# Dealing a skinny fp32 projection to four column groups of TensorE's array

## The chip, the core and the metric

The kernel runs on one core of a Trainium2 chip. The metric is the device time of one execution in microseconds. Before the change three runs gave 2735.04, 2735.30 and 2738.25 us, median 2735.3. A profile of one further execution shows what each engine did and when: TensorE (PE, with its weight loads as PEld), VectorE (DVE), ScalarE (ACT), GpSimd (POOL) and SyncE (SP), which issues the DMAs.

## The reference

Two layers of a hybrid backbone over 2048 latent tokens and 256 context tokens of width 1024. Each layer normalises its input, modulates it by vectors that come from a conditioning vector, and runs windowed attention (8 heads) and a bidirectional mLSTM (4 heads) side by side, followed by one output projection:

```python
sc = jax.nn.silu(c)
scc = jax.nn.silu(c_ctx)
for l in range(DEPTH):
    mod_x = jnp.split((sc @ w_ada[l] + b_ada[l])[:, None, :], 3, axis=-1)
    mod_c = jnp.split(scc @ w_ada[l] + b_ada[l], 3, axis=-1)
    x, ctx = hybrid_layer(x, ctx, mod_x, mod_c, tables, norm_g[l], w_in[l], ...)
...
    xn = rmsnorm(x, norm_g) * (1 + scale_x) + shift_x
    cn = rmsnorm(ctx, norm_g) * (1 + scale_c) + shift_c
```

The change is in the two products with `w_ada[l]`, 1024 x 3072 in fp32: two rows (`sc` and `scc`) times a large matrix, once per layer.

## The kernel before

The kernel records its instructions through a planner (`Plan`): generators yield while something they need is not there yet by the planner's own model, and the loop `run_until` lets the next one go. `cost` holds the planner's price of every instruction; `stream` gives each large job a priority and a weight, and among equal priorities the job that has used the least planned TensorE time for its weight goes first. So the planner's prices set the order in which all engines' instructions stand, and each engine then runs them in that order, waiting on semaphores. All instructions carry the line of the helper `op`, L228 in the profile, so the rows are told apart by tiles and not by lines.

`ada` computes the modulation. Its columns are cut into chunks: 8 chunks of 256 columns in the first stretch (shift and scale of layer 0, buffers `wada`, of which there are three), and then 32 chunks of 128 columns (the gate of layer 0, all of layer 1, buffers `g`, shared with other work). For each chunk, `loads` issues the load of the weights `wt` (1024 rows as eight k-tiles of 128) and of the bias `bt`. Then eight matmuls, one for each k-tile, accumulate in one PSUM bank `b`: the stationary operand is `self.sc[:, k, :]`, 128 rows by two columns (latent and context), the moving operand is the k-tile of `wt`, 128 rows by 256 or 128 columns, and the result is two partitions of the bank. The generator `rows` then adds the bias on DVE, for the scale also multiplies by the norm's gain, takes a maximum for the scaling of fp16 splits (`gm`), and stores the row to `modD` in DRAM, from where it is loaded later, broadcast to 128 partitions (`kT`, `V`).

In the first stretch nothing else of size can run: the normalised input needs the modulation, and the loads of `x` (`xt<-in_x`) wait until the chunks are loaded and the context's rows are stored and loaded back. After that the 32 smaller chunks run as a stream of their own beside two large ones, the attention (`alpha`) and the mLSTM (`beta`). All work on layer 1 beyond its modulation starts after layer 0's output projection.

Of the kernel before, what the change touches and what calls it, by code (L numbers as in the profile page):

```python
# [10 lines left out]
ALU = mybir.AluOpType  # L11
# [4 lines left out]
KT = D // P  # L16
# [37 lines left out]
def _isap(v):  # L54
    return hasattr(v, "ap") and hasattr(v, "offset")


def _free(v):
    n = 1
    for d in v.shape[1:]:  # L60
        n *= d
    return n
# [33 lines left out]
def _move(out, in_):  # L96

    b = 2 if out.dtype == F16 else 4
    for d in out.shape:
        b *= d  # L100
    r = max(min(_run(out), _run(in_), 4096), 4)
    return b / r * (10 + 0.0447 * r) / 16e3


def _base(out, in_):

    if out.space == bass.MemoryType.DRAM:
        return 1.5
    return 1.9 if in_.name.startswith("in_") else 3.6
# [14 lines left out]
class Plan:  # L124
# [29 lines left out]
    def cost(self, e, name, a, kw):  # L154
        n = _free(a[0])
        if e == "E":
            if name == "transpose":
                return 0.003 + (n / 1200.0 if a[1].dtype == F32 else 0.03), 0.1
            if kw["rhs"].dtype == F32:
                return max(4 * n, 512) / 2400.0 + 0.005, 0.1  # L160
            return max(n, 64) / 2400.0 + 0.0027, 0.1
        if e == "Q":
            if name == "dma_start_transpose":
                return 1.2 + max(n - 512, 0) * 0.00045, 1.9 + n / 128 * 128 * 25e-3 / 16
            return 0.49, _base(a[0], a[1]) + _move(a[0], a[1])
        if name == "tensor_reduce":
            n = _free(a[1])
        cols = sum(_isap(v) and _free(v) == 1 for v in (*a[2:], kw.get("scale"), kw.get("bias")))
        if e == "S":
            base = 0.05 if a[1].space == bass.MemoryType.PSUM else 0.11  # L170
            return base + n / 1200.0 + 0.08 * cols + (0.11 if "accum_out" in kw else 0.0), LAT
        if e == "G":
            if name == "memset" or name == "tensor_copy":
                return 0.12 + n / 1600.0, LAT
            if name == "tensor_scalar":
                return 0.18 + n / 1080.0, LAT
            return (0.55 if a[-1] == ALU.pow else 0.14) + n * 2.1e-3, LAT
        if name == "reciprocal":
            n *= 8
        if name == "tensor_tensor_reduce":  # L180
            return 0.25 + n / 960.0, LAT
        if name == "tensor_copy" and a[0].dtype == F16:
            n /= 2
        return 0.065 * (1 + min(cols, 2)) + n / 960.0, LAT

    def op(self, e, name, fn, a, kw):
# [4 lines left out]
        if name == "tensor_tensor_reduce":  # L191
            outs.append(ins.pop())
        cost, lat = self.cost(e, name, a, kw)
        t = self.clk[e]
        for v in ins:
# [8 lines left out]
        if e == "Q":  # L204
            t = max(t, self.lanes.pop(0))
        elif e == "G" or (e == "V" and _two(a, kw)):
            other = self.port["V" if e == "G" else "G"]
            for p, q in other:
                if p <= t < q:
                    t = q  # L210
            self.port[e] = self.port[e][-5:] + [(t, t + cost)]
# [145 lines left out]
class Kern(Plan):  # L357
# [240 lines left out]
    def ada(self, l, parts, width, tags):  # L598

        A, Q, V = self.A, self.Q, self.V  # L600
        c = self.c
        nch = D // width
        if 1 not in parts:
            yield from self.need(("kv", l))
        else:
            gm = c.tile([2, 2, 8], F32, tag="gm", name="gm")
            V.memset(gm, 0.0)
        todo = [(j, n) for j in parts for n in range(nch)]
        ready = []

        def loads():
            for i, (j, n) in enumerate(todo):
                c0 = j * D + n * width
                if tags[0] == "g":
                    yield from self.room("g", 3)
                wt = yield from self.get(tags[0], [P, KT, width])
                Q.dma_start(wt, A["w_ada"][l, :, c0:c0 + width].rearrange("(k p) c -> p k c", p=P))
                bt = yield from self.get(tags[1])
                Q.dma_start(bt[:, 0], A["b_ada"][l:l + 1, c0:c0 + width].to_broadcast([2, width]))
                if j == 1:  # L620
                    Q.dma_start(bt[:, 1], A["norm_g"][l:l + 1, n * width:(n + 1) * width].to_broadcast([2, width]))
                ready.append((wt, bt))
                yield True
            if l == 0:
                self.done.add("ada in")

        def rows(j, n, ps, bt):
            row = yield from self.get(tags[2])
            yield from self.till(ps)
            V.tensor_tensor(row, ps[:2, :width], bt[:, 0], ALU.add)  # L630
            self.put(ps)
            if j == 1:
                V.scalar_tensor_tensor(row, row, 1.0, bt[:, 1], ALU.add, ALU.mult)
            self.put(bt)
            if j < 2:
                V.tensor_reduce(gm[:, 1 - j, n:n + 1], row, AX.X, ALU.max, apply_absolute_value=True)
            jj = {1: 0, 0: 1, 2: 2}[j]
            yield from self.till(row)
            for s in range(2):
                Q.dma_start(self.modD[l][s][jj][:, n * width:(n + 1) * width], row[s:s + 1])  # L640
            self.put(row)
            self.done.add(("mod", l, jj, n))

        self.spawn(loads())
        for i, (j, n) in enumerate(todo):
            while not ready:
                yield None
            wt, bt = ready.pop(0)
            yield from self.till(wt)
            ps = yield from self.get("b")  # L650
            for k in range(KT):
                self.mm(ps[:2, :width], self.sc[:, k, :], wt[:, k, :], start=(k == 0), stop=(k == KT - 1))
            self.put(wt)
            self.spawn(rows(j, n, ps, bt))
            yield True
            if (j, n) == (0, nch - 1):
                yield from self.need(*[("mod", l, a, b) for a in range(2) for b in range(nch)])
                bnd, mx = self.held(), self.held()
                V.memset(bnd, 0.0)
                m2 = self.col(2)  # L660
                V.tensor_reduce(m2[:2], gm, AX.X, ALU.max)
                V.tensor_tensor(bnd[:2], m2[:2, 0:1], m2[:2, 1:2], ALU.add)
                V.tensor_scalar(bnd, bnd, 32.0, None, ALU.mult)
                yield from self.pmax(bnd, mx)
                self.sx[l] = c.tile([P, 1], F32, name=f"sx{l}")
                self.ix[l] = c.tile([P, 1], F32, name=f"ix{l}")
                self.scale_of(mx, 1, self.sx[l], self.ix[l])
                self.done.add(("sx", l))
        yield from self.need(*[("mod", l, {1: 0, 0: 1, 2: 2}[j], n) for j, n in todo])
        if 0 in parts:  # L670
            self.done.add(("ada", l))
        if 2 in parts:
            self.done.add(("gate", l))
# [1361 lines left out]
```

## Time and profile before

| | us |
|---|---|
| median of three runs | 2735.3 |
| the profiled execution | 2737.6 |
| its span, first to last instruction | 2735.8 |
| PE busy in the span | 2445.0 (89%) |
| DVE busy | 1871.7 (68%) |
| ACT busy | 1496.5 (55%) |
| POOL busy | 1505.3 (55%) |

The page gives these shares; since the kernel runs in stages, the rows below are mostly of single stretches. A timeline row merges instructions of one kind that follow each other on one engine: start, length, engine, line, operation, output and input tiles, shapes, count, and in brackets the idle time before it with what ended it. A matmul's recorded length includes its way through the array, so consecutive ones overlap in the record; the pace of a run of n is its length less one record's, divided by n - 1, or the distance between the starts of two runs divided by the count.

### The profile page before, as it was taken

What the parts mean: (1) busy time and instruction counts of PE and PEld (TensorE: products, weight loads), DVE (VectorE), ACT (ScalarE), POOL (GpSimd) and SP (SyncE); (2) the same over time, 40 slices, a digit from 0 to 9 for tenths busy, and PEclk for the clock granted to TensorE, in tenths of its full rate; (3) what the DMA queues carried; (4) which work ended last, traced back from release to release, by engine and by line L of the source; (5) the groups of instructions that cost most, each with busy time, mean ns of one, the idle gap of its engine ahead of it and who ended that gap; (6) DMA issues with size and microseconds to landing.
All of it is one profiled execution on the core that took longest, in us unless ns stands there. A gap on an engine that the chain in (4) does not pass through costs nothing. (4 is left out here: it accounts for less than half of the span.)

```text
span 2735.8 us, 64752 instructions
## 1 busy us (share of the span) xinstructions
PE 2445.0 (89%) x23650; PEld 1883.3 (69%) x23650; DVE 1871.7 (68%) x4817; ACT 1496.5 (55%) x3788; POOL 1505.3 (55%) x2832
## 2 busy tenths in 40 slices
PE   6699999999999999886898799998899899978887
PEld 2567887789778968773454468968876896866333
DVE  4888666856685667576666687777659768666554
ACT  2446675657666756572222357756666676665111
POOL 1846477547765854574222664783786387357000
PEclk9799999999999999998999999999999999989998
DMA  8354873476457643687786437726754763466554
GB/s 269 96 157 98 162 142 86 117 157 135 85 141 157 137 109 91 127 194 207 183 197 189 111 96 158 144 58 126 153 117 104 140 126 83 98 150 152 159 161 123
DMA packets 822447, 376.16 MB, mean 137 GB/s; under 512 B 492536, under 2 KB 800240, under 8 KB 821104
## 3 DMA queue, kind: packets, MB, share of 16 engines
q1 hardware_dynamic: 822128, 372.02, 58.7%
q8 instruction: 186, 3.05, 0.5%
q14 instruction: 133, 1.09, 0.1%
HBM read 198.99 MB, written 57.56 MB: 94 GB/s over the span
## 5 line engine op out<-in xcount | busy, mean ns | idle before, releaser
L228 PEld LDWEIGHTS <-xt 128*128 128x128 f16 x12144 | 911.6, 99 | 303.6 <-issue 76.2
L228 PE MATMUL b<-woz,xt 128*128 128x256 f16 (+2 forms) x3872 | 496.1, 277 | 26.7 <-DMA xt<-xt 13.2
L228 PE MATMUL b<-xt,wqk 128*128 128x512 f16 (+1 forms) x1824 | 388.0, 363 | 2.7 <-DVE wqk L228 2.7
L228 POOL TENSOR_TENSOR held<-held,mhalf 128x1 f32<-128x1 f32 x200 | 117.8, 590 | 333.9 <-DVE held L228 321.4
L228 PEld LDWEIGHTS <-wqk 128*128 128x128 f16 x1824 | 174.8, 98 | 160.6 <-issue 4.3
L228 ACT ACTIVATE d<-d,smx,un 128x640 f32<-128x640 f32 (+2 forms) x272 | 223.9, 823 | 95.9 <-DVE smx L228 85.6
L228 DVE SCALAR_TENSOR_TENSOR ph<-d,ph 128x640 f16<-128x640 f32 (+2 forms) x272 | 211.9, 780 | 92.2 <-ACT ph L228 89.8
L228 PE MATMUL b<-wa,xt 128*128 128x128 f16 (+1 forms) x3352 | 259.6, 226 | 3.6 <-DVE held L228 1.1
L228 POOL TENSOR_TENSOR p<-p 128x128 f32<-128x128 f32 x272 | 127.2, 470 | 214.6 <-ACT p L228 165.4
L228 PE MATMUL b<-wv,xt 128*128 128x128 f16 x3456 | 229.7, 219 | 16.1 <-DVE s L228 6.2
L228 DVE CUSTOM_DVE_ANT_0 d<-d,mask 128x640 f32<-128x640 f32 (+1 forms) x240 | 195.9, 816 | 30.4 <-PE d L228 29.5
L228 POOL TENSOR_TENSOR g<-g,mb 128x512 f32<-128x512 f32 (+1 forms) x152 | 194.5, 1280 | 36.5 <-ACT g L228 21.5
L228 PE MATMUL b<-xt,xt 128*128 128x512 f16 x768 | 178.5, 395 | 33.6 <-ACT d L228 20.4
L228 PE MATMUL d<-ks,toz 128*128 128x256 f16 (+1 forms) x1568 | 189.2, 257 | 20.6 <-DVE toz L228 15.7
L228 POOL TENSOR_TENSOR toz<-toz,cs 128x256 f32<-128x256 f32 x160 | 119.7, 769 | 154.8 <-DMA cs<-in_rope 113.4
L228 PE MATMUL b<-xt,wa 128*128 128x256 f16 x1632 | 201.1, 273 | 2.3 <-DVE held L228 1.0
L228 ACT ACTIVATE ph<-d 128x640 f16<-128x640 f32 (+2 forms) x272 | 182.5, 671 | 14.3 <-DMA pp<-ph 7.2
L228 DVE TENSOR_TENSOR toz<-toz 64x256 f16<-64x256 f32 (+2 forms) x234 | 144.5, 618 | 60.7 <-ACT toz L228 28.5
L228 PEld LDWEIGHTS <-toz 128*128 128x128 f16 x1568 | 146.7, 99 | 48.7 <-DVE toz L228 19.7
L228 PEld LDWEIGHTS <-wa 128*128 128x128 f16 x1696 | 161.8, 98 | 25.3 <-issue 2.4
L228 DVE SCALAR_TENSOR_TENSOR g<-g,cw 128x512 f32<-128x512 f32 (+1 forms) x152 | 149.8, 986 | 23.3 <-POOL g L228 20.6
L228 DVE SCALAR_TENSOR_TENSOR s<-s,gc,b 128x129 f32<-128x129 f32 x272 | 94.0, 346 | 84.7 <-ACT p L228 49.3
(243 smaller groups left out, 5195.4 us busy)
## 6 DMA issues: line engine op xcount, KB each, us to landing
mb<-mD SPq DMA_DIRECT2D x136, 256.0 KB
g<-in_w_in SPq DMA_DIRECT2D x60, 512.0 KB
cs<-in_rope SPq DMA_DIRECT2D x80, 256.0 KB
mixD<-p SPq DMA_DIRECT2D x272, 64.0 KB
g<-mixD SPq DMA_DIRECT2D x34, 512.0 KB
g<-in_w_ada SPq DMA_DIRECT2D x32, 512.0 KB
g<-in_x SPq DMA_DIRECT2D x24, 512.0 KB
cfD<-s SPq DMA_DIRECT2D x136, 64.5 KB
```

Of the source, the lines that this page charges most:

```text
L228: fn(*a, **kw)
```

## The change

The eight k-tiles of a chunk no longer accumulate in one place. k-tile k goes to partitions g and g + 1 of the bank, g = 32 (k mod 4), that is to one of four column groups of TensorE's array: k-tiles 0 to 3 start the four sums, 4 to 7 end them. DVE, which added the bias to one row pair, now adds the other three row pairs one after the other. In the planner, an fp32 matmul whose stationary operand has two columns is priced at a quarter. The number of matmuls stays; DVE gets three adds more for each of 40 chunks, 120 in all.

```diff
@@ cost
             if kw["rhs"].dtype == F32:
-                return max(4 * n, 512) / 2400.0 + 0.005, 0.1
+                t = max(4 * n, 512) / 2400.0 + 0.005
+                return t / 4 if _free(kw["lhsT"]) == 2 else t, 0.1
@@ ada, rows
             V.tensor_tensor(row, ps[:2, :width], bt[:, 0], ALU.add)
+            for g in (32, 64, 96):
+                V.tensor_tensor(row, ps[g:g + 2, :width], row, ALU.add)
             self.put(ps)
@@ ada
             for k in range(KT):
-                self.mm(ps[:2, :width], self.sc[:, k, :], wt[:, k, :], start=(k == 0), stop=(k == KT - 1))
+                g = 32 * (k % 4)
+                self.mm(ps[g:g + 2, :width], self.sc[:, k, :], wt[:, k, :], start=(k < 4), stop=(k >= 4))
```

The lower price and the adds change the order on all engines. On SyncE's queue in the first stretch (`wada` is a chunk's weights, `bt` its bias, `modD<-row` the store of a finished row pair), before:

```order
L228 DMA wada_212<-in_w_ada 128x8x256
L228 DMA bt_233<-in_b_ada 2x256
L228 DMA bt_233<-in_norm_g 2x256
L228 DMA wada_236<-in_w_ada 128x8x256
L228 DMA modD_98<-row_214 1x256
L228 DMA modD_101<-row_214 1x256
L228 DMA bt_269<-in_b_ada 2x256
L228 DMA wada_271<-in_w_ada 128x8x256
```

and after:

```order
L229 DMA wada_212<-in_w_ada 128x8x256
L229 DMA bt_227<-in_b_ada 2x256
L229 DMA bt_227<-in_norm_g 2x256
L229 DMA modD_98<-row_214 1x256
L229 DMA modD_101<-row_214 1x256
L229 DMA wada_241<-in_w_ada 128x8x256
L229 DMA bt_266<-in_b_ada 2x256
L229 DMA modD_98<-row_243 1x256
L229 DMA modD_101<-row_243 1x256
L229 DMA wada_279<-in_w_ada 128x8x256
```

The fifth and the sixth load (the second and third here) now stand behind the stores of the first and the second chunk's rows; the fifth stood ahead of them before.

On DVE, in the stream of the attention and the mLSTM, around the rows of a chunk (`row<-b,bt` adds the bias, `p`, `s` and `col` belong to the other streams), before, at the last chunk:

```order
L228 SCALAR_TENSOR_TENSOR s<-s,gc,b 128x129
L228 STREAM_SHUFFLE toz<-toz 128x256
L228 TENSOR_TENSOR row<-b,bt 2x128
L228 ISA d,col_18626<-d,mask 128x640
L228 ISA col_18626 128x1
```

and after, at two of the later chunks:

```order
L229 TENSOR_TENSOR row<-b,bt 2x128
L229 TENSOR_TENSOR row<-b,row 2x128 x3
L229 SCALAR_TENSOR_TENSOR p<-b,un,p 128x128
L229 SCALAR_TENSOR_TENSOR p<-toz,b 128x128
L229 SCALAR_TENSOR_TENSOR s<-s,gc,b 128x129
L229 SCALAR_TENSOR_TENSOR col_7023<-b,gc 128x2
L229 TENSOR_TENSOR col_7023<-b,col_7023 128x2
L229 RECIPROCAL col_7023<-col_7023 128x2
L229 SCALAR_TENSOR_TENSOR p<-toz,b 128x128
L229 TENSOR_TENSOR row<-b,bt 2x128
L229 TENSOR_TENSOR row<-b,row 2x128 x3
```

Chunks that stood far apart now follow each other with little between them. In the whole order the last chunk's bias add was row 1921 of DVE's 4517 and is now row 859 of 4553; on PE the last chunk stood at row 18,446 of 42,526 and now stands at row 6,579 of 42,530. From a place within layer 0's output projection on (the first `b<-wa,xt` of 128x512, at about 1305 us of the trace before) PE's order is the same in both to the end.

## Rows read from the trace of the kernel before

**Rows 1.** The page: span, and each engine's busy time, share and instructions.

```profile
span 2735.8 us, 64752 instructions
PE 2445.0 (89%) x23650; PEld 1883.3 (69%) x23650; DVE 1871.7 (68%) x4817; ACT 1496.5 (55%) x3788; POOL 1505.3 (55%) x2832
```

**Rows 2.** Busy time of each engine by stretch; the first row names the columns.

```profile
core 0: us, PE busy (x) PEld busy (x) DVE busy (x) ACT busy (x) POOL busy (x), PEclk, DMA share, GB/s
...
150.00:310.00 160.00, 151.30 (x1679) 119.16 (x1677) 128.47 (x326) 96.66 (x221) 75.36 (x96) 1.00 0.58 133
310.00:470.00 160.00, 151.88 (x1511) 128.84 (x1509) 101.05 (x328) 102.31 (x297) 121.07 (x262) 0.99 0.63 127
470.00:1110.00 640.00, 614.73 (x6749) 511.22 (x6747) 435.83 (x1228) 411.81 (x1099) 384.24 (x715) 0.99 0.56 124
...
1305.00:2735.00 1430.00, 1277.81 (x11653) 935.32 (x11650) 977.10 (x2384) 734.56 (x1820) 726.17 (x1380) 0.97 0.58 135
1700.00:2300.00 600.00, 563.18 (x6073) 475.04 (x6071) 431.75 (x1211) 403.20 (x1088) 416.13 (x800) 0.99 0.59 120
```

**Rows 3.** PE's waits, 150 to 1110 us: releaser, total us, times, longest.

```profile
PE b L228 <- DVE p L228: 9.4, 11, 2.7
PE b L228 <- DVE s L228: 4.8, 5, 2.4
PE b L228 <- DVE toz L228: 4.4, 5, 2.2
PE b L228 <- DVE row L228: 4.3, 1, 4.3
```

**Rows 4.** Tile `sc`: record ns min/median/max, first and last start us, form.

```profile
L228 PE MATMUL b<-g,sc x512: 269/273/417, 55.7 to 1105.3; 128*2 128x128 f32 x171
...
L228 PE MATMUL b<-wada,sc x128: 377/379/631, 13.4 to 44.3; 128*2 128x256 f32 x128
```

**Rows 5.** Timeline of PE in layer 0: start us, length us, tiles, count.

```profile
1097.01 1.01 PE L228 MATMUL b<-vp,pp 128*128 128x128 f16 x20
1097.86 1.06 PE L228 MATMUL b<-wv,xt 128*128 128x128 f16 x16
...
1103.64 1.91 PE L228 MATMUL b<-g,sc 128*2 128x128 f32 x16
1105.48 0.72 PE L228 MATMUL d<-ks,toz 128*128 128x256 f16 x6
```

**Rows 6.** Timeline of PE in the first 60 us.

```profile
13.45 9.48 PE L228 MATMUL b<-wada,sc 128*2 128x256 f32 x32
...
23.41 3.62 PE L228 MATMUL b<-wada,sc 128*2 128x256 f32 x16
...
27.21 17.43 PE L228 MATMUL b<-wada,sc 128*2 128x256 f32 x80
...
55.69 4.54 PE L228 MATMUL b<-g,sc 128*2 128x128 f32 x24 [8.97 <-DMA g<-in_w_ada]
```

**Rows 7.** Timeline of SyncE's queue in the first 60 us.

```profile
30.85 0.39 SPq L228 DMA_DIRECT2D wada<-in_w_ada  x1
...
34.31 0.40 SPq L228 DMA_DIRECT2D wada<-in_w_ada  x1
...
53.91 5.29 SPq L228 DMA_DIRECT2D xt<-in_x  x8
```

**Rows 8.** Timeline of DVE: last chunk of 256 columns, first of 128.

```profile
44.93 0.41 DVE L228 TENSOR_TENSOR row<-b,bt 2x256 f32<-2x256 f32 x1 [2.85 <-DMA modD<-row]
45.37 0.41 DVE L228 TENSOR_REDUCE gm<-row 2x1 f32<-2x256 f32 x1
...
59.30 0.28 DVE L228 TENSOR_TENSOR row<-b,bt 2x128 f32<-2x128 f32 x1 [8.71 <-PE b L228]
59.62 1.20 DVE L228 SCALAR_TENSOR_TENSOR row<-row,bt 2x128 f32<-2x128 f32 x1
```

**Rows 9.** Stretches as in rows 2; the last number is GB/s.

```profile
13.00:18.00 5.00, 4.96 (x12) 1.54 (x13) 1.00 (x6) 1.44 (x2) 0.00 (x0) 1.00 1.09 398
...
24.00:30.00 6.00, 6.00 (x29) 2.26 (x27) 2.86 (x14) 0.00 (x0) 3.11 (x10) 1.00 0.84 258
```

## The prediction

> **What bounds the kernel now.** I read four views. First the page: TensorE (PE) is busy 89% of the 2735.8 us span, VectorE (DVE) 68% [rows 1]. An average over stages says little, so next the table by stretch: from 150 to 1110 us PE is busy 95 to 96% [rows 2], and what it waits for there is small and spread; the four longest entries are all DVE, 22.9 us together [rows 3]. In that stretch a microsecond off PE is nearly a microsecond off the time. Then the rows of `sc`, the tile that every projection loads as weights: 512 records for 32 chunks of 128 columns and 128 for 8 chunks of 256, all before 1106 us [rows 4]. So each fp32 matmul stands in the trace as **two** load-and-matmul pairs, and a chunk is 16. Last the stretch from 12 to 60 us, where the first 8 chunks gate everything: the loads of `x` are issued at 53.91, after the last chunk's rows are stored [rows 6, 7].
>
> How far the change reaches is plain from the built order: from the place that stands at about 1305 us before, TensorE's order is the same instruction for instruction to the end. So 1430 us [rows 2] should not move, and everything below lies before that.
>
> **A, the first 8 chunks.** The last 5 run as one block: 17.43 us for 80 records, (17.43 - 0.379)/79 = 0.216 apart, 3.45 a chunk [rows 4, 6]. Only three `wada` buffers exist, and the load issued at 34.31 comes just after the chunk begun at 27.21 + 3.45 = 30.66 has ended at 34.11 [rows 6, 7]. So a faster chunk starts the next load earlier. Below I put a faster chunk at about 2.0 us, and then the loads bound: 1.05 MB at the best rate seen, 398 GB/s, is 2.6 us, at 258 GB/s 4.1 [rows 9]; I take 2.8, nearer to the first, since the second was met while PE set the pace. Five chunks times 3.45 - 2.8 = 3.3 us, and the three before them end about 3 x 1.4 = 4.1 us earlier: 7.4. Against it, the last row gets three more adds of 2 x 256 before the reduction and the stores that follow: 0.45 apart [rows 8], +1.35. Two loads now stand behind stores of rows on SyncE's queue, as the order shows; those rows end some 2.3 us (five DVE steps of 0.45) after chunks that are two places earlier, which a load at 2.8 us a chunk covers. If PE gets no faster only the 1.35 stays. **A = -6, bounds +1.4 and -9.**
>
> **B, the other chunks on PE.** A chunk of 128 columns goes from 1103.64 to the next instruction at 1105.48: 1.84 us. Its records are (1.91 - 0.273)/15 = 0.109 apart, so 16 take 1.74, and 0.10 is lost on the way back to full-width matmuls [rows 4, 5]. No row of before has two matmuls in different column groups, so whether they run side by side is unknown. Bounds from rows: at worst they stay 0.109 apart, nothing gained. At best one pair is issued every 0.042 us, as in the attention matmuls that follow one another at (1097.86 - 1097.01)/20 [rows 5]: 16 x 0.042 + 0.109 + 0.10 = 0.87.
>
> Between them stands what I take. The two records of one matmul go to the same group, and the diff puts matmul after matmul, so in order the list is group 0, 0, 1, 1, 2, 2, 3, 3. If records start in order, the second of each pair still waits 0.109 for the first, and only the step to the next group is cheap: between 0 and 0.042. Eight such steps give 8 x 0.109 + 0.109 + 0.10 = 1.08, or 8 x 0.151 + 0.10 = 1.30; I take the middle, 1.19, a gain of 0.65. (The 256-column chunk by the same sum is about 2.0 for 3.45.) Two of the 32 chunks stand behind a load that PE waits 8.97 us for [rows 6] and gain nothing; 30 x 0.65 = 19.5.
>
> The Trainium skill bears on this in two ways. "TensorE: Matmul & The Clock Gate", section "Part 3: Packing small matmuls", says that matmuls start and end strictly in program order even where tiles overlap; by that rule the gain is the 19.5 above. "TensorEngine Tiling (Array Packing)", section "Key Properties", says that tiles run loads and matmuls in parallel, and its table gives up to 4x for four column groups; by that the chunk comes near 0.87 and B is -29. Both would be seen only after the change; the trace shows neither.
>
> What may come back: the chunks also move. The order now has all of them done within the first 6,600 of PE's 42,530 rows, before it was 18,400. They were filler between the attention and mLSTM streams. Layer 1, from 1700 to 2300, runs these streams without chunks, and there PE is 93.9% busy against 96.0% from 470 to 1110 [rows 2]. The difference over 640 us is 14 us at most; since the filler's own work is not lost but done earlier, in place of waits there, I take +3. **B = -16.5, bounds 0 (or +14, if nothing overlaps and the filler is missed) and -29.**
>
> **C, the adds.** 30 chunks x 3 adds x 0.32 [rows 8] = 29 us more for DVE, and one of the four PSUM banks `b` is held a microsecond longer each time. DVE has room: 128.5 of 160 us from 150 to 310, 101 of 160 after it, 436 of 640 later [rows 2]. But the chunks come denser: by the order some 13 fall into 150 to 310, where 5 or 6 stood; 13 x 0.96 for the adds and some 7 x 0.8 for the moved rows make +18, which takes DVE there from 80 to about 91%. Queued behind the adds on DVE are evacuations that PE waits for (`p`, `s`, `toz`: 18.6 us in all [rows 3]). If such waits grow by a quarter that is 5; hidden it is 0, fully exposed 29. **C = +5.**
>
> **D, transfers.** 24 loads of `w_ada` come earlier into a stretch that has DMA busy 58 to 63% [rows 2]; nothing of before waits there for them in sum, and I price it at 0, inside the range.
>
> **Sum.** -6 - 16.5 + 5 = -17.5. The profiled execution took 2737.6 us (1.8 outside its span); the median of the runs is 2.3 lower, 2735.3. So 2735.3 - 17.5 = 2718.
>
> **The rivals.**
> - *Four groups at once.* The second record of a pair waits in its own group while the next group's starts. A falls a little further, to -7.5, since loads bound it; B is -29 + 4; C +6 since rows come faster: -26.5, 2709. For it: distinct groups need not share anything, and records of one group 0.109 apart are set by streaming alone. Against: no row shows two matmuls starting together.
> - *No overlap; the adds cost.* If fp32 records of different groups follow one another at 0.109, PE gains nothing, and what is left is A = +1.4, C = +5 and the missed filler, +2: +8, 2744. It decides as soon as a chunk gains less than about 0.2 us (30 x 0.2 pays for C and the filler). For it: every fp32 stream in the rows runs at exactly one streaming time per record. This is the one on the slow side: an engine that is 80% busy in the densest stretch gets the work.
> - *A change of group costs what a change of tile shape does.* The 0.10 at a chunk's end, paid at 8 changes a chunk, is 30 x 0.8 = 24, and with the adds and A the time is near 2772. Against: position is not shape; all of these matmuls already have the small shape.
> - *The change does not do what it says* would look like the second: rows in the same group, DVE adding what it need not.
>
> **How the numbers follow.** Chances: pairs by two (my forecast) 0.40, four at once 0.22, no overlap 0.32, costly changes 0.06. About 0.2%, 5.5 us, is what a measurement here can tell. The reordering before 1305 us can move the time by some 8 us either way in each case, so the forecast's 17.5 stays beyond 5.5 in nine of ten, four at once nearly always, while no overlap splits: slower two parts, same one, a trace of faster. Faster 0.36 + 0.21 + 0.01 = 0.58; same 0.04 + 0.01 + 0.10 = 0.15; slower 0.21 + 0.06 = 0.27. The range for 8 in 10 goes from four at once with little filler lost, 2701, to no overlap with C at twice its price, 2748. The forecast's own range is 2706 to 2732.
>
> **What would show it.** In the trace after: starts of `b<-g,sc` records alternating 0.109 and under 0.05 (forecast), all under 0.05 (four at once), or 0.109 throughout (none); a chunk of 1.1 to 1.3 us; the block of 256-column chunks with waits for loads in it and `x` issued at about 48 rather than 53.91; DVE about 90% busy around 150 to 310; PE's waits for DVE up by about 5; the stretch after the first `b<-wa,xt` of 128x512 still 1430 long. Wrong would be a spacing that does not change, or a gain on PE that returns as waits for DVE.

## The result, and the profile after

The changed kernel took **2749.4 us** (median; 2746.7 to 2754.2), the kernel before, beside it, 2736.4: a ratio of **1.0053** [1.0038, 1.0067]. It is half a per cent slower. The forecast was 2718, faster, with a range up to 2748. The profiled execution took 2746.7 us. In every fence below the columns are those of the rows of the same view ahead of the prediction.

The page of after, beside [rows 1], and its line of the granted TensorE clock in 40 slices:

```profile
span 2744.9 us, 64897 instructions
...
PE 2409.4 (88%) x23650; PEld 1854.0 (68%) x23650; DVE 1919.5 (70%) x4937; ACT 1497.6 (55%) x3788; POOL 1511.4 (55%) x2832
...
PEclk6799999999999999998999999999999999989999
```

PE is 35.6 us less busy than before, in a span 9.1 us longer. So the deal did save work on TensorE, and the saving did not reach the end. The stretches, beside [rows 2]:

```profile
150.00:310.00 160.00, 141.34 (x1563) 106.59 (x1564) 135.25 (x338) 87.31 (x201) 74.26 (x93) 0.95 0.59 131
310.00:470.00 160.00, 142.65 (x1659) 123.82 (x1659) 106.14 (x376) 96.40 (x282) 99.94 (x235) 0.95 0.81 163
470.00:1110.00 640.00, 601.26 (x6539) 495.97 (x6527) 449.66 (x1227) 418.50 (x1111) 411.24 (x746) 0.98 0.54 112
...
1305.00:2735.00 1430.00, 1285.42 (x11733) 942.36 (x11733) 974.12 (x2385) 733.96 (x1821) 723.63 (x1375) 0.97 0.59 136
1700.00:2300.00 600.00, 563.15 (x6097) 476.28 (x6095) 428.61 (x1213) 403.49 (x1099) 417.88 (x811) 0.99 0.60 122
```

PE's share from 150 to 470 us fell from 95 to 88 and 89%, the granted clock there from 0.99 and more to 0.95, and the DMA share of the second stretch rose from 0.63 to 0.81. Layer 1 (1700 to 2300) is as it was. PE's waits from 150 to 1110 us, beside [rows 3]:

```profile
PE b L229 <- DVE p L229: 20.6, 20, 2.9
PE b L229 <- DVE held L229: 10.5, 6, 4.1
PE b L229 <- DMA g<-in_w_ada: 7.1, 2, 4.4
PE b L229 <- DVE s L229: 6.8, 7, 1.8
PE b L229 <- DVE row L229: 5.6, 7, 1.7
```

The wait for `p` doubled, `held` and the chunks' own loads are new among the long ones. One chunk on PE and its rows on DVE, beside [rows 5, 8]:

```profile
308.77 0.62 PE L229 MATMUL b<-g,sc 128*2 128x128 f32 x16
309.32 1.07 PE L229 MATMUL b<-wv,xt 128*128 128x128 f16 x16
```

```profile
309.46 0.28 DVE L229 TENSOR_TENSOR row<-b,bt 2x128 f32<-2x128 f32 x1 [0.23 <-PE b L229]
309.77 0.93 DVE L229 TENSOR_TENSOR row<-b,row 2x128 f32<-2x128 f32 x3
```

A chunk takes 0.55 us to the next instruction, where it took 1.84. The three adds are 0.93. The tile `sc`, beside [rows 4]:

```profile
L229 PE MATMUL b<-g,sc x512: 269/272/422, 52.9 to 497.4; 128*2 128x128 f32 x171
L229 PE MATMUL b<-wada,sc x128: 378/631/635, 13.8 to 37.9; 128*2 128x256 f32 x128
```

All chunks are over by 498 us, and the median record of the first eight is 631 ns long, not 379: most of them run at the lower of the two clocks. The line of the clock begins with 6 here (above, slices of 69 us); before it began with 9:

```profile
PEclk9799999999999999998999999999999999989998
```

**Where the time went.** From the starts of PE's records I made an account of three stretches, cut at matmuls that every version has: from the first `b<-xt,wqk` (156 us) to the 361st `b<-vp,pp` (a product of the attention), on to the 1081st, and on to the place from which PE's order is the same in both kernels. Each form of matmul has a usual distance to the next start, its median at the full clock. These sums are "work" (and "chunk" for `b<-g,sc`); what a distance exceeds its usual by is "half" as far as one more usual distance goes while the records show the lower clock, and otherwise "wait". It is worked out from the trace, not a view of it.

```
                 chunks in it   length us              chunk us          wait us           half-clock us
before            10, 18, 1     343.2  560.5  244.8    18.1  32.8  1.8   21.4  34.9  53.3   1.4   5.7  10.6
after             28,  0, 0     373.5  541.9  244.8    15.2   0    0     44.0  46.9  54.3  11.4   8.4  11.7
```

Other work is 968 us in both. Chunks fell by 37.5; waits rose by 35.6 and half-clock time by 13.8: +11.9, which is the +11.7 of the lengths but for rounding. From the common place to the end of the span it is 1430.7 us before and 1428.2 after. So all of the loss lies where the order differs, and of the 49 us that came back nearly three quarters are waits. (One execution of each kernel.)

### The profile page after: what moved, and what is told of

Its sections match the earlier page's. It is cut to its first block, busy times and chain, and to the rows that moved or that the text cites. A ratio compares the mean times of both kernels' runs of the same rounds, so it can differ in the third digit from the quotient of the medians.

```text
span 2744.9 us, 64897 instructions
## 1 busy us (share of the span) xinstructions
PE 2409.4 (88%) x23650; PEld 1854.0 (68%) x23650; DVE 1919.5 (70%) x4937; ACT 1497.6 (55%) x3788; POOL 1511.4 (55%) x2832
## 5 line engine op out<-in xcount | busy, mean ns | idle before, releaser
L229 PE MATMUL b<-xt,xt 128*128 128x512 f16 x768 | 178.5, 395 | 33.6 <-ACT d L229 17.5
```

Source lines behind the costliest of these rows:

```text
L229: fn(*a, **kw)
```

## The experiments

Two things changed together: the deal (with its adds), and the order of all engines, through the planner's price. The experiments take them apart. "Order" below is that of all instructions on all engines, the adds aside. Each ratio is against the kernel before, run beside it.

### The deal in the old order

Against the changed kernel, the planner has the old price again and does not know of the adds:

```diff
-                t = max(4 * n, 512) / 2400.0 + 0.005
-                return t / 4 if _free(kw["lhsT"]) == 2 else t, 0.1
+                return max(4 * n, 512) / 2400.0 + 0.005, 0.1
...
-                V.tensor_tensor(row, ps[g:g + 2, :width], row, ALU.add)
+                self.nc.vector.tensor_tensor(row, ps[g:g + 2, :width], row, ALU.add)
```

> The deal to four column groups and the three adds, but in the order of before: the planner keeps the old price and does not know of the adds, so every engine has the instructions of before in the order of before, with three adds behind each bias add. Theory 'order' (what the deal saves on PE is lost because the lower price packs the chunks together between 250 and 500 us): PE keeps about 30 of the 38 us that the dealt chunks save, and the time is 2700 to 2715. Theory 'adds' (DVE's three adds and the bank held longer cost it): 2736 to 2750. Theory 'clock' (dealt chunks leave PE too little to do and the granted clock falls): 2725 to 2745 with more cold stretches than before.

Ratio 1.0013 [0.9998, 1.0028]. The deal with its adds, in the order of before, gives no gain that can be told from none, although the chunks are as short as in after. The time lies where the theories 'adds' and 'clock' had it, and not in the 2700 to 2715 of 'order': the saving is lost in the old order too. Of this kernel's waits from 150 to 1110 us the longest are, against [rows 3]:

```profile
PE b L228 <- DVE p L228: 15.1, 17, 2.5
PE b L228 <- DVE row L632: 8.4, 5, 6.1
PE b L228 <- DVE held L228: 7.4, 8, 3.8
PE b L228 <- ACT toz L228: 6.4, 4, 4.1
```

### The new order without the deal

The planner sees the changed kernel, and what is issued is one group and no adds:

```diff
-                self.mm(ps[g:g + 2, :width], self.sc[:, k, :], wt[:, k, :], start=(k < 4), stop=(k >= 4))
+                one = lambda out, lhsT, rhs, start, stop: self.nc.tensor.matmul(
+                    ps[:2, :width], lhsT=lhsT, rhs=rhs, start=(k == 0), stop=(k == KT - 1))
+                self.op("E", "matmul", one, (ps[g:g + 2, :width],),
+                        dict(lhsT=self.sc[:, k, :], rhs=wt[:, k, :], start=(k < 4), stop=(k >= 4)))
```

> The order of the changed kernel with the work of before: the planner still counts a quarter price and three adds, but all eight k-tiles accumulate in one group and no adds are issued. Theory 'order': as slow as the changed kernel plus what its chunks save, 2765 to 2790. Theories 'adds' and 'clock': the order is harmless, 2733 to 2745.

Ratio **1.0134** [1.0108, 1.0160], the slowest of all, in the range of the theory 'order'. So the order alone costs 1.3%, and in this order the deal with its adds is worth 1.0053 - 1.0134 = -0.8%. The waits that were new in after, from 150 to 1110 us, are here without a shorter chunk:

```profile
PE b L229 <- DVE p L229: 16.3, 15, 2.6
PE b L229 <- DVE held L229: 10.4, 6, 3.8
PE b L656 <- DMA g<-in_w_ada: 5.1, 2, 3.2
```

So `held` and most of the growth in `p` (9.4 before, 16.3 here, 20.6 in after) and in the loads come with the order and not with what the deal takes off PE.

### The changed kernel without the adds

```diff
-                V.tensor_tensor(row, ps[g:g + 2, :width], row, ALU.add)
+                self.op("V", "tensor_tensor", lambda *a, **kw: None, (row, ps[g:g + 2, :width], row, ALU.add), {})
```

(The rows then hold one partial sum of four.)

> The changed kernel in its own order with the three adds planned but not issued, so three of four partial sums are left out. Theory 'adds': 2710 to 2725. Theory 'order': 2740 to 2750, within 8 us of the changed kernel.

Ratio 1.0036 [1.0022, 1.0051]; by the medians of the ratios the adds cost 0.17%, some 5 us, though the intervals of the two overlap. The loss stays without them.

### The deal in the old order, without adds; the adds alone

The first is the first experiment with the loop of adds removed (again one partial sum of four is kept). The second is the kernel before with three more adds for each chunk, into a spare tile:

```diff
+            more = row
+            for _ in range(3):
+                self.nc.vector.tensor_tensor(self.spare[:, :width], ps[:2, :width], more, ALU.add)
+                more = self.spare[:, :width]
```

> The order of before and the deal, without the three adds, so that three of four partial sums are left out: what the deal alone is worth where nothing else moves. The same order with the adds came out 3.5 us above before although dealt chunks take 38 us less of PE. Theory 'adds' (DVE's adds eat the gain): 2698 to 2710. Theory 'pace' (the other engines' chains set the pace of the old order, and PE only arrives earlier and waits): 2724 to 2734, PE's waits up by 20 or more.

> The kernel before with three more adds on DVE behind each bias add, of the same shapes from the same bank, into a tile that nobody reads: the adds without the deal. Theory 'adds': 2755 or more. Theory 'pace': the adds fall partly on the path, since in this order other engines are close to it: 2736 to 2744.

0.9955 [0.9937, 0.9972] and 1.0027 [1.0014, 1.0040]. In the old order the deal alone is worth 0.45%, some 12 us, of the 37 us that PE saves; the adds then cost 0.27% by themselves and 0.58% beside the deal (1.0013 - 0.9955). A microsecond off PE was worth a third of one here. The first time is in the range of the theory 'pace'; the second, 2745.5 us, is just above it and well short of the 2755 of 'adds'.

### Spreading the chunks again

`stream` gives the job that has used the least planned TensorE time for its weight the next turn. At a quarter of the price and the old weight the chunks get four times their turns. So I lowered the weight, first by the same factor:

```diff
-   self.stream(self.ada(i, (1, 0, 2) if i else (2,), P, ("g", "bt", "row")), 2, 43.0 if i else 14.0)
+   self.stream(self.ada(i, (1, 0, 2) if i else (2,), P, ("g", "bt", "row")), 2, 10.75 if i else 3.5)
```

and then to a half (21.5, 7) and an eighth (5.375, 1.75).

> The changed kernel with the weights of the two chunk streams at a quarter too (10.75 for 43, 3.5 for 14), so that the planner spreads the chunks over layer 0 as before. Theory 'order' in its narrow form (chunks packed together): 2700 to 2720. If any reordering costs, whatever the spread: 2730 to 2750. Theory 'adds': 2740 to 2750.

> The changed kernel with the weights of the chunk streams at a half (21.5 and 7), so that the last chunk stands between its place in the changed kernel and its place in the version at a quarter, which ran in 2720. If packing the chunks is what costs: 2728 to 2742. If that version was only a lucky order: anywhere from 2715 to 2755, no step between the two.

> The same with weights at an eighth (5.375 and 1.75); the chunks stand about as late as at a quarter. If spreading is what counts, the time is that of the quarter: 2714 to 2728. If the order's luck counts more, it is off by more than 8 us either way.

```
weight              1        1/2      1/4      1/8
last chunk begins   497 us   685 us   1090 us  1089 us
ratio               1.0053   0.9978   0.9959   0.9927
95%                 1.0038   0.9967   0.9946   0.9906
                    1.0067   0.9990   0.9972   0.9947
```

At a half, 13 chunks lie in the first stretch of the account and 15 in the second, all before 690 us; at a quarter and an eighth the last stand at 1090 us. The loss turns into a gain as the chunks are spread. At an eighth the kernel takes 2718.5 us and beats before and after. (The quarter and the eighth have nearly as many chunks in each stretch, 11, 16, 1 and 11, 15, 2, and differ by 0.32% in the ratio and by 2 us in the median: the spread does not settle that much.) The eighth's row for `sc`:

```profile
L229 PE MATMUL b<-g,sc x512: 269/272/418, 52.6 to 1089.6; 128*2 128x128 f32 x171
```

### The best order without the deal

The edit is that of the second experiment, on the kernel with an eighth of the weight.

> The order of the version with weights at an eighth (2718), with all k-tiles in one group and no adds issued. If that version's gain comes from the deal: 2736 to 2750, slower than it by 18 or more. If it was the order alone: 2715 to 2725.

Ratio 1.0009 [0.9997, 1.0021]. This settles the gain of the last section: it is the deal's, 0.9927 - 1.0009 = -0.8%, and not that of a better order. The four corners and the old order:

```
order               one group, no adds    dealt, adds    the deal is worth
of before           1 (before)            1.0013         +0.1%
of after            1.0134                1.0053         -0.8%
an eighth's         1.0009                0.9927         -0.8%
packed order costs  +1.25%                +1.26%         (after's order against an eighth's)
```

The packed order costs the same with and without the deal, some 34 us. Here is where, in the pair without the deal, whose profiled executions are 27.3 us apart. The order of after first, in windows that end at the same matmuls (the 361st and the 1081st `b<-vp,pp`), then an eighth's:

```profile
150.00:543.00 393.00, 370.55 (x3718) 291.06 (x3716) 266.46 (x744) 220.55 (x567) 221.50 (x389) 0.99 0.61 133
543.00:1084.00 541.00, 507.98 (x5484) 426.14 (x5483) 371.95 (x1045) 358.70 (x966) 356.18 (x674) 0.97 0.56 116
```

```profile
150.00:511.00 361.00, 341.03 (x3503) 272.29 (x3501) 263.75 (x716) 219.52 (x567) 223.51 (x393) 1.00 0.57 123
511.00:1057.00 546.00, 521.18 (x5695) 436.43 (x5693) 376.26 (x1072) 356.92 (x966) 353.46 (x669) 1.00 0.64 131
```

In the first window PE is 94% busy in both, and 17 more chunks make it 32 us longer. In the second PE has 13.2 us less to do, and the window is only 5 us shorter: it takes 541 us without chunks and 546 with 15 of them. By the account:

```
                           chunks in it   length us              chunk us          wait us           half-clock us
order of after, no deal     28,  0, 0     383.5  541.2  245.8    51.2   0    0     25.2  43.2  55.7   3.3  11.2  11.2
an eighth's, no deal        11, 15, 2     349.1  546.3  246.4    19.9  27.2  3.7   21.1  35.6  51.4   0     1.3  11.6
an eighth's, dealt          11, 15, 2     346.7  532.8  244.4     5.7   7.8  1.1   29.5  37.7  50.3   3.5   5.1  13.3
of before, dealt, adds      10, 18, 1     347.1  556.7  242.6     5.2   9.6  0.6   33.2  53.7  51.1   6.7   7.0  11.7
```

Where chunks are taken out, waits (+7.6) and the lower clock (+9.9) fill 17.5 us of the 27.2 they leave, and the other streams stand there with 4.7 us more of their own work, which the first window has less of. Where they are put in, they cost their full length and 7.4 us of waits and lower clock more (less 4.3 of other work). In after itself, against an eighth's dealt order, the sizes are the other way about: in the first stretch 9.5 us more of chunks, and 22.4 more of waits and lower clock.

### Other causes looked at: the loads, and filler as such

Transfers are packed too (a DMA share of 0.81). Here the loads of the 32 small chunks bring one k-tile of eight, 64 KB for 512, and all eight matmuls read it, once in the order of after and once in the kernel before (the modulation uses only the first k-tile of its weights in both):

```diff
+                n1 = 1 if tags[0] == "g" else KT
+                self.op("Q", "dma_start", lambda o, i: Q.real.dma_start(o[:, 0:n1], i[:, 0:n1]),
+                        (wt, A["w_ada"][l, :, c0:c0 + width].rearrange("(k p) c -> p k c", p=P)), {})
```

> The changed kernel in its own order, but each of the 32 smaller chunks loads only its first k-tile, 64 KB in place of 512, and all eight matmuls read that one; the modulation is wrong by that. If the transfers of w_ada, 30 of them packed between 150 and 500 us, set the pace there: 2715 to 2730, DMA busy there back to 60%. If DVE and the order of the other work set it: 2742 to 2752.

> The control: the kernel before with the same small loads, in its own order (the modulation is wrong as there). The loads are spread out there, so within 6 us of before, 2728 to 2740; if it gains as much as the changed kernel does, the transfers cost everywhere and packing is not the reason.

1.0017 [1.0007, 1.0027] and 0.9970 [0.9958, 0.9982]: against 1.0053 and 1 the small loads give 0.36% and 0.30%, and of the 0.53% between the two kernels 0.47 stay (1.0017 - 0.9970; the first, 2740.7 us, lies between its two forecasts). Packing the transfers is not what the order costs.

Last, if the chunks are worth most as filler, they should go best where nothing else can run: the stream at priority 3, behind the attention and the mLSTM.

```diff
+   self.stream(self.ada(i, (1, 0, 2) if i else (2,), P, ("g", "bt", "row")), 3)
```

> The changed kernel with the two chunk streams one priority below the attention and the mLSTM, so that a chunk stands only where the planner finds neither able to go on: chunks as filler and nothing else. If PE's waits after the last chunk come from missing filler: 2710 to 2725, as the versions with small weights. If filler does not matter: 2735 to 2750.

1.0003 [0.9992, 1.0014], where the expectation had it for filler that does not matter. Its chunks are spread nearly like an eighth's (11, 17 and 0 in the three stretches for 11, 15 and 2, the last at 960 us), and it is 0.76% slower. Its waits and half-clock time are 34.1 us in the first stretch and 64.2 in the second, against 33.0 and 42.8. So spreading is not all: which instructions of the other streams stand between the chunks decides over some 20 us, and what in that order it is I have not found.

## Why the prediction was wrong, step by step

Two of its steps failed: that work taken off PE is time, and the +3 for the chunks that move. The measured +0.53%, some 14 us where -17.5 was forecast, is made of +1.34% for the order and -0.81% for the deal and its adds in that order.

**What bounds it.** "In that stretch a microsecond off PE is nearly a microsecond off the time" was read from PE being 95 to 96% busy [rows 2]. It is the reading that failed. In the order of before 37 us off PE gave 12 without adds and none with them. With the chunk shorter, PE comes sooner to the same results and waits for them: the account of the old order, dealt, shows waits of 33.2 and 53.7 us for 21.4 and 34.9, and the same account without the adds some 26 and 53, so most of this is not the adds. My reading of that: the order is fixed ahead by a planner that priced a chunk at its old length, and so the other engines' results were laid to be there when PE was done with it. For it speaks that the same deal is worth 0.8% in both orders that were planned with the low price, and without its adds 0.98% in after's order (1.0036 - 1.0134) against 0.45% in the old one. That this is the reason is not shown: both orders were planned with the adds too, and no run separates that. In the spread order of an eighth, 36 us of chunks off PE (50.8 to 14.6 in the account) came out as 0.82%, some 22 us. A high busy share showed that little was waited for; it did not show that nothing was close behind.

**A, the first chunks: -6; right for PE, more than half given back on DVE.** They are bound by their loads, as was said (starts 2.8 us apart), and most run at the lower clock:

```profile
13.78 1.89 PE L229 MATMUL b<-wada,sc 128*2 128x256 f32 x16
16.62 1.89 PE L229 MATMUL b<-wada,sc 128*2 128x256 f32 x16 [0.95 <-DMA wada<-in_w_ada]
...
36.69 1.89 PE L229 MATMUL b<-wada,sc 128*2 128x256 f32 x16 [1.65 <-DMA wada<-in_w_ada]
43.65 0.48 PE L229 MATMUL b<-ident,held 128*128 128x128 f32 x1 [5.08 <-DVE held L229]
```

```profile
40.82 0.41 DVE L229 TENSOR_TENSOR row<-b,bt 2x256 f32<-2x256 f32 x1 [0.48 <-DMA modD<-row]
41.26 1.33 DVE L229 TENSOR_TENSOR row<-b,row 2x256 f32<-2x256 f32 x3
42.63 0.41 DVE L229 TENSOR_REDUCE gm<-row 2x1 f32<-2x256 f32 x1
```

```profile
50.86 0.35 SPq L229 DMA_DIRECT2D kT<-modD  x1
51.26 5.08 SPq L229 DMA_DIRECT2D xt<-in_x  x8
```

The eight are over at 38.58 us, 6.1 earlier than before [rows 6]. DVE, still at the rows of the two chunks before it, begins the last chunk's bias add at 40.82, 4.1 earlier than before [rows 8]; its adds take 1.33 more, as forecast, and the reduction comes 2.7 earlier. So `x` is issued at 51.26, 2.65 earlier than before [rows 7], where about 6 was forecast: the term counted the adds of the last row and left out the rows, with their own adds, that stand before it on DVE. The first `b<-xt,wqk` comes at 156.4 for 156.6. Here too order and deal work against each other: without the deal that matmul comes at 159.5 in the new order; with the deal, in the old order, at 154.1 with the adds and 151.9 without. (These are single executions, worth a few microseconds.)

**B, the chunks on PE: gain 0.65 each, mis-sized; it is 1.29.** The rival "four groups at once" had the mechanism. Its bound of 0.87 us a chunk (0.88 by its own terms) was itself too long, since I took 0.042 between two issues from attention matmuls. The starts of the 16 records of the chunk at 308.77, as the trace has them:

```
ns after the first: 0 8 14 20   109 115 122 129   217 224 230 238   327 334 339 346
```

Four start within 20 ns, and the next four one streaming time, 0.109 us, after the first. So a chunk is 4 x 0.109 plus about 0.11 at its end. The chance of 0.22 for this case was too low, and the argument that the second record of a pair holds back the next group was wrong. On the Trainium skill's two places: "TensorEngine Tiling (Array Packing)", section "Key Properties", says that tiles run in parallel, and the trace agrees, at its full factor of four. "TensorE: Matmul & The Clock Gate", section "Part 3: Packing small matmuls", says that starts stay in program order; the records do not say which group each belongs to, so no run here shows whether they do, but the gain that I drew from it, 0.65, is not what the trace shows.

**B, what may come back: +3, bounded by 14; this is the term that set the sign.** The order alone cost some 37 us (1.0134), and the order of after against an eighth's, both dealt, 34. I had taken the chunks' work as "done earlier, in place of waits there". There were few waits there: PE was 94% busy from 150 us on, and in the new order without the deal the first stretch grew by 40.3 us for 33.1 of chunks. In the second stretch, without its 32.8 of chunks, it was only 19.3 shorter than before. There waits and the lower clock took 13.8 us back, which is the bound of 14 that I had drawn from layer 1's missing 2%; I took 3 for want of belief in it, and left out the first stretch (5.7 more of the same), the first 156 us (2.9) and the work behind the common place (3.6). Under it lay the larger mistake: the price of one instruction moves the order of all, and I gave that 3 us and a spread of 8.

**C, the adds: +5.** About right in the order of after (0.17%, 5 us) with 0.31 us for an add, as forecast. In the old order, beside the deal, they cost 0.58%, 16 us; the waits of PE there are mostly for DVE. DVE is 85% busy from 150 to 310 us, where 91 was forecast: 10 chunks begin there, not 13.

**D, transfers at 0,** holds for the difference of the two kernels: small loads give as much before as after, within the intervals. Layer 1's 1430 us hold too.

**The rivals.** The slow one, "no overlap", gave 2744 and was near the time by another mechanism: the groups do overlap. The true one, an order made worse by the new price, stood as a term of 3 us and not as a rival. The sentence on what would be wrong, "a gain on PE that returns as waits for DVE", is the nearest to what happened, but it is half of it: in the old order the gain does return so (`p` 9.4 us [rows 3] to 15.1), while of the 20.6 in after 16.3 are there without any gain on PE.

## What to carry to other kernels

Where a planner's price sets the order, a change of price is a change of its own: try the faster work in the old order, the new order with the old work, and only then both. A busy share of 95% does not say that an engine sets the pace. In an order fixed ahead for the old durations, two thirds of what was saved on one engine did not reach the time here, and the account shows it as waits for the others and as time at the lower clock. Filler that is made cheaper should keep its spread: here lowering its weight by eight turned a loss of 0.5% into a gain of 0.7%. Spread alone is not enough: as the lowest priority the chunks were spread as well and gained nothing.

## What the runs showed of the hardware

- Fp32 matmuls of two columns in four column groups run fully side by side: four records start within 20 ns, and the 16 of a chunk of 128 columns take 0.55 us where they took 1.84. The steps between such starts are 5 to 8 ns, and no other price of changing the group can be seen.
- PE was granted the lower clock (1.2 GHz) for longer. The first eight chunks, with waits of 0.85 to 1.65 us for loads between them, ran with records of 631 ns for 379, and from 156 us to the common place half-clock time rose from 17.7 to 31.5 us, in the account above. In the old order with the deal it was 25.4, in the new order without it 25.7. It is part of why work taken off PE did not come off the time.
- Loading an eighth of the bytes for 32 chunks, with everything else in place, gives 0.30% in the kernel before, some 8 us. Its trace shows one long wait for such a load, 8.97 us [rows 6]; with small loads the first `b<-xt,wqk` comes 3.6 us earlier in the profiled execution, and where the rest comes from I have not looked at.
